# An encoder trunk of two layers on one core: the mLSTM gates as columns of the first value group, two norm rows through DRAM, and one PSUM tile per token half in the last block

## Chip, cores and metric

The kernel runs on one core of a Trainium2 chip. The metric is the device time of one execution in microseconds (us); lower is better.

## What is computed

The reference is a hybrid encoder of two layers over 256 tokens of width 2048, float32 in and out. Cut to what the change touches:

```python
for layer in range(2):
    h = rms_norm(x, norm_mix[layer])
    if layer % 2 == 0:   # pooling + grouped-query attention, one input and one output projection
        ...
    else:                # mLSTM, 8 heads of 256, forward and backward
        proj = h @ w_in_c                      # 2048 x (4 * 2048 + 32)
        q, k, v, o = four blocks of 2048 columns
        gates = proj[..., 4 * 2048:] + b_gate  # 32 columns: (i, f) x 2 directions x 8 heads
        # per head and direction: scores weighted with exp(cumulative gates), running maximum,
        # normalised, summed over both directions, RMSNorm per head, times sigmoid(o)
        mixed = y @ w_out_c
    x = x + mixed
    x = x + conv_ffn(rms_norm(x, norm_ffn[layer]), ...)   # 2048 -> 2 * 5632, conv of width 3, SiLU gate, 5632 -> 2048
```

## The kernel before

**Precision.** Every large product is done in float32r with split operands: a value is stored as a high part and a rest, and a product is high x high + high x rest + rest x high, accumulated in PSUM.

**Weights.** `Stream` (line 65) brings the weights in chunks of 128 x 1024 floats, in the order in which they are used: SP loads a chunk (line 78) up to five ahead into six buffers, ScalarE (ACT) writes its high part (line 87), VectorE (DVE) the rest (line 88), two chunks ahead into four buffers.

**Activations.** The residual `x` lies with tokens on partitions, in two halves t of 128 tokens. `Norm` (line 226) makes the transposed input `xx` of the next layer from it: after each 512 columns of the residual are final, `add` takes their squares on ACT and, some microseconds of PE work later, `block` transposes them on TensorE (PE, line 251) and writes high part and rest with the gain (lines 263, 266). The scale 1/rms is not multiplied into `xx` but into the products. `finish` (line 275) makes it in two shapes: `rcol`, one number per token with tokens on partitions (a power on GpSimd (POOL), line 207, and a few short steps on DVE), and `R`, the same numbers as a row on every partition: two diagonal matrices on DVE (`dg`, line 284), a product with ones on PE (`npr`, line 287) and a copy (line 289). There are four norms, numbered 0 to 3, two for each layer.

**Groups of products.** `stat_group` (line 292) keeps weights stationary and streams `xx`; per tile of 128 input rows k it issues two matmuls of 512 columns and two of 256. `mov_group` (line 331) keeps `xx` stationary and streams the weights, `width` columns at a time, six matmuls per k; it returns a PSUM tile from the pool `mm`, which has two. Small work of the heads (transposes, scores) uses the pool `ps` with four tiles.

**Order.** PE's instructions stand in program order, written by hand. `Weave` (line 109) puts the small steps between the matmuls of the groups: a step is a generator that says after how many microseconds of PE work it may go on, and every matmul group ticks that clock. Outside the first stage the order of ACT, DVE, POOL and SP is made by the framework's scheduler.

**mLSTM layer** (line 657). For each pair of heads hp: the values (`mv`, a moving group of 512 columns, line 841), scaled with `rcol` on ACT (line 844) and split; then for each of its heads q and k (`mq`, `mk`, stationary groups, scaled with `R` in `scaled`, line 735), and the output gates (`mo`). `gates` (line 686), added to the weave behind the first value group, has 32 matmuls of its own (`gps`): the 32 gate columns, spread to rows 0 to 103, stationary, in 16 tiles k with 512 and 256 streamed columns. Their weights are a load of their own, split on ACT and DVE into a tile cleared by POOL (lines 665 to 673). The gate rows [104, 256] get `R` and the bias, and then logarithms, running sums and maxima; the row for the heads goes to DRAM (`gd`, line 719) and each head fetches its part as a broadcast (`G`, line 757); two other rows are turned into columns on PE (`cols`, line 725). A head starts when `gate` is filled. In the attention layer `k_block` (line 548) runs `finish` of norm 0 as part of its steps; a power for the scales of k (`ry_qk`, line 207) stands between its two halves (line 436), and `R` is read by the pool groups (line 576).

**FFN layer** (line 870). `down` of the last chunk ends, for the last 512 columns, in `down_end` (line 903): one PSUM tile of both token halves; the last two k go half by half, the second half in two pieces of 256 columns, each added to the residual (line 925) and stored (line 926) as it is done.

Of the kernel before, what the change touches and what calls it, by code (L numbers as in the profile page):

```python
# [16 lines left out]
P = 128  # L17
# [47 lines left out]
class Stream:  # L65
# [8 lines left out]
    def load(self, pieces=1):  # L74
        i, n = self.n_load, CH * P // pieces
        w = self.wpool.tile([P, CH * P], F32, tag="w", name=f"w{i}")
        for c in range(0, CH * P, n):
            self.nc.sync.dma_start(w[:, c : c + n], self.srcs[i][:, c : c + n])
        self.w[i] = w, n
        self.n_load += 1  # L80

    def split(self, then=None):
        i = self.n_split
        w, n = self.w.pop(i)
        hl = self.spool.tile([P, 2, CH * P], F32R, tag="hl", name=f"hl{i}")
        for c in range(0, CH * P, n):
# [68 lines left out]
def trunk(ctx: ExitStack, tc: tile.TileContext, gx, xT, xn, call, catt, cml, wgate, weights, out):  # L155
# [12 lines left out]
    sm1 = pool("small1", 1)  # L168
    mmp = pool("mm", 2, space=PSUM)
# [56 lines left out]
    class Norm:  # L226


        def __init__(self, n):
# [3 lines left out]
            self.blocks, self.R = 0, None  # L233
# [41 lines left out]
        def finish(self):  # L275
# [5 lines left out]
            yield 2.5  # L281
            dg = sm1.tile([P, 2, P], F32, tag="dg", name=f"dg{n}")
# [48 lines left out]
    def mov_group(act, name, width=512, before=None, after=None):  # L331

        ps = mmp.tile([P, 2, width], F32, tag="mm", name=name)
        per = CH * P // width
        hl = None
        for k in range(KT):
# [9 lines left out]
            for t, i, j in terms:  # L346
                first, last = k == 0 and (width == 512 or t == 0), k == KT - 1 and (width == 512 or t == 1)
                mm(ps[:, t, :], src[:, i, t * P : t * P + P], hl[:, j, c : c + width],
                   first and i + j == 0, last and i == 1)
# [307 lines left out]
    def mlstm_layer(norm, nxt):  # L657
        with ExitStack() as es:
# [10 lines left out]
            g.memset(wgp.bitcast(F32), 0.0)  # L669
# [460 lines left out]
```

## Time and profile before

| | us |
|---|---|
| median of three runs | 2212.0 (2211.6 to 2212.02) |
| profiled execution | 2211.96 |
| its span, first to last instruction | 2209.7 |
| PE busy in the span | 2203.7 |
| DVE, ACT, POOL busy | 1527.5, 1169.1, 27.7 |

The granted clock of PE is 1.00 over the run. In the rows of the profile, L200 is the helper that issues matmuls, so groups are told apart by the tile that they write: `mv<-hl,xx` is the value group. A row of the timeline gives start, length, engine, line, operation, output and input, shapes, count, and in brackets the idle time before it with what ended it. PEld is the loading of the stationary operand, which overlaps PE. A matmul's length includes the drain that the next one overlaps, so lengths of single matmuls do not add up to time on PE.

### The profile page before, as it was taken

To read this page: it belongs to the slowest core of one execution; us is meant where nothing else is said; L and a number is where in the kernel's file an instruction comes from. 1 tells how busy PE (TensorE), PEld (TensorE's weight loads), DVE (VectorE), ACT (ScalarE), POOL (GpSimd) and SP (SyncE) were. 2 spreads that over 40 slices of the span, in tenths; PEclk is the share of its full clock that TensorE was granted. 3 is DMA by queue.
4 is the path that set the end of the run, shared out by engine and by line. 5 is a ranking of instruction groups with operands and counts; after the bars stand their busy time and mean duration, and the time that the engine had idled before them with its cause. 6 is when DMAs were issued, how large, how long until landed. Compare 5 with 4: busy or idle time off the path is not lost.

```text
span 2209.7 us, 30530 instructions
## 1 busy us (share of the span) xinstructions
PE 2203.7 (100%) x11656; PEld 1886.9 (85%) x11656; DVE 1527.5 (69%) x2180; ACT 1169.1 (53%) x1662; POOL 27.7 (1%) x36
## 2 busy tenths in 40 slices
PE   9999999999999999999999999999999999999999
PEld 7888888888888888888888889888888888888887
DVE  7686677776766767666777677667777677676764
ACT  7665555554554545455455554555555455454542
POOL 0020000000000000000000000000000000000000
PEclk9999999999999999999999999999999999999999
DMA  9455566656566566655565555655565656656564
GB/s 340 157 165 173 175 191 190 191 188 194 187 193 189 188 194 189 200 181 164 172 200 180 183 180 165 187 178 188 188 191 189 197 185 193 188 190 192 190 193 141
DMA packets 117876, 415.45 MB, mean 188 GB/s; under 512 B 12986, under 2 KB 15458, under 8 KB 117730
## 3 DMA queue, kind: packets, MB, share of 16 engines
q1 hardware_dynamic: 114512, 409.50, 58.1%
q10 hardware_dynamic: 3218, 4.01, 0.7%
q8 instruction: 91, 1.49, 0.3%
q14 instruction: 55, 0.45, 0.1%
HBM read 411.31 MB, written 2.14 MB: 187 GB/s over the span
## 4 chain that ended last, share of the span: by engine, by line
PE 99%; DMA 0%; DVE 0%; SPq 0%; ACT 0%; issue 0%
PE up L200 44%; PE dn L200 21%; PE op L200 8%; PE mk L200 4%; PE mq L200 4%; PE mo L200 4%; PE mv L200 4%; PE qproj L200 3%; PE pool L200 1%; PE vproj L200 1%; PE kproj L200 1%; PE end L200 1%; PE qk L200 1%; PE av L200 1%; PE xt L251 0%; PE ov L200 0%
## 5 line engine op out<-in xcount | busy, mean ns | idle before, releaser
L88 DVE TENSOR_TENSOR hl<-w,hl 128x1024 fp32r<-128x1024 f32 (+1 forms) x770 | 938.3, 1219 | 467.9 <-ACT hl L87 466.3
L87 ACT CAST hl<-w 128x1024 fp32r<-128x1024 f32 (+1 forms) x769 | 805.9, 1048 | 674.8 <-PE dn L200 240.9
L200 PE MATMUL up<-xx,hl 128*128 128x512 f32 (+1 forms) x5632 | 984.2, 337 | 0.0
L200 PEld LDWEIGHTS up<-xx,hl 128*128 128x128 f32 x5632 | 857.9, 188 | 125.9
L200 PE MATMUL dn<-hl,g 128*128 128x512 f32 x2064 | 471.3, 389 | 0.0
L200 PEld LDWEIGHTS dn<-hl,g 128*128 128x128 f32 x2064 | 386.2, 188 | 79.5
L356 ACT COPY tb_up<-up 128x512 f32<-128x512 f32 x88 | 51.7, 587 | 153.9 <-PE up L200 153.9
L357 DVE TENSOR_TENSOR tb_up<-up,tb_up 128x512 f32<-128x512 f32 x88 | 60.9, 691 | 97.0 <-ACT tb_up L356 97.0
L892 ACT ACTIVATE y<-tb_up,cst 128x256 f32<-128x256 f32 x176 | 96.4, 595 | 47.1 <-DVE tb_up L888 47.1
L200 PE MATMUL mk<-xx,hl 128*128 128x512 f32 (+1 forms) x512 | 92.4, 338 | 0.0
L200 PE MATMUL mq<-xx,hl 128*128 128x512 f32 (+1 forms) x512 | 92.0, 337 | 0.0
L200 PE MATMUL mo<-hl,xx 128*128 128x512 f32 (+1 forms) x480 | 91.6, 348 | 0.0
L200 PE MATMUL op<-hl,cat 128*128 128x512 f32 x384 | 91.6, 393 | 0.0
L200 PE MATMUL mv<-hl,xx 128*128 128x512 f32 x384 | 89.6, 391 | 0.0
L200 PE MATMUL op<-hl,mcat 128*128 128x512 f32 x384 | 89.5, 392 | 0.0
L200 PEld LDWEIGHTS mq<-xx,hl 128*128 128x128 f32 x512 | 79.3, 188 | 11.7
L200 PEld LDWEIGHTS mk<-xx,hl 128*128 128x128 f32 x512 | 79.1, 188 | 11.5
L200 PEld LDWEIGHTS mo<-hl,xx 128*128 128x128 f32 x480 | 76.5, 189 | 10.6
L200 PEld LDWEIGHTS mv<-hl,xx 128*128 128x128 f32 x384 | 71.7, 188 | 14.8
L200 PEld LDWEIGHTS op<-hl,mcat 128*128 128x128 f32 x384 | 71.4, 188 | 14.6
L200 PEld LDWEIGHTS op<-hl,cat 128*128 128x128 f32 x384 | 70.9, 188 | 14.1
L893 DVE SCALAR_TENSOR_TENSOR y<-tb_up,cst,y 128x255 f32<-128x255 f32 x176 | 76.7, 477 | 0.0
(211 smaller groups left out, 1285.1 us busy)
## 6 DMA issues: line engine op xcount, KB each, us to landing
w<-in_up SPq DMA_DIRECT2D x352, 512.0 KB, 4.0
w<-in_dn SPq DMA_DIRECT2D x176, 512.0 KB, 4.0
w<-in_m_in SPq DMA_DIRECT2D x128, 512.0 KB, 4.0
w<-in_a_in SPq DMA_DIRECT2D x46, 512.0 KB, 4.2
w<-in_a_out SPq DMA_DIRECT2D x32, 512.0 KB, 3.5
w<-in_m_out SPq DMA_DIRECT2D x32, 512.0 KB, 3.5
x<-in_xn SPq DMA_DIRECT2D x4, 512.0 KB, 9.3
G<-gd ACTq DMA_DIRECT2D x16, 128.0 KB, 4.9
```

The source lines that it names most:

```text
L87: (self.nc.vector.tensor_copy if i + c == 0 else self.nc.scalar.copy)(hl[:, 0, c : c + n], w[:, c : c + n])
L88: self.nc.vector.tensor_sub(hl[:, 1, c : c + n], w[:, c : c + n], hl[:, 0, c : c + n].bitcast(F32))
L200: pe.matmul(out_, lhsT, rhs, start=start, stop=stop, skip_group_check=True)
L356: a.copy(tb, ps[:, :, 1, :])
L357: v.tensor_add(tb, ps[:, :, 0, :], tb)
L892: a.activation(y[:, j, :], u[:, j, :], AF.Identity, scale=cw(tl, 1), bias=cw(tl, 3))
L893: v.scalar_tensor_tensor(y[:, j, 1:S], u[:, j, 0 : S - 1], cw(tl, 0), y[:, j, 1:S], ALU.mult, ALU.add)
```

## The change

- **Gates in the first value group.** The first value group (512 columns) becomes two moving groups: one of 288 columns, the first head's 256 value columns and the 32 gate columns, and one of 256, the second head's values. The tile of the first has 512 columns for each token half, of which 288 are used. Its weights come as chunks of 3 k x 288 = 864 columns (the last has one k, 288). `gates` then scales the gate columns with `rcol` on ACT into a cleared tile `gn`, turns them with two transposes on PE (`gtr`), and adds the bias; the rest of the chain is the same, and its wait before `cols` is 16 us of PE work instead of 13. The gates' own weights, their load, split, memset and 32 matmuls go. The clock steps of `finish` are 6 us instead of 8, and the weave is run until `rcol` exists before the evacuation.
- **Norm rows.** For norms 0 and 2, `R` is made by two DMAs on POOL's queue: `rcol` to a DRAM row, and the row back as a broadcast to 128 partitions. For norms 1 and 3 it stays as it was.
- **Last block.** `down_end` uses two PSUM tiles of the pool `ps`, one for each token half; the second half is done in one piece of 512 columns.

```diff
     def load(self, pieces=1):
-        i, n = self.n_load, CH * P // pieces
+        i = self.n_load
+        width = self.srcs[i].shape[-1]
+        n = width // pieces
...
             self.rcol = rsqrt(s2, 2, 1.0 / D, f"n{n}")
             yield 2.5
+            if n % 2 == 0:
+                rr = dram.tile([2, P], F32, tag="rr", name=f"rr{n}")
+                g.dma_start(rr.rearrange("t p -> p t"), self.rcol)
+                R = sm1.tile([P, S], F32, tag="R", name=f"R{n}")
+                g.dma_start(R.rearrange("p (t q) -> p t q", t=2), rr.unsqueeze(0).to_broadcast([P, 2, P]))
+                self.R = R
+                return
             dg = sm1.tile([P, 2, P], F32, tag="dg", name=f"dg{n}")
...
-            wgf = t1p.tile([P, KT, 4, MH], F32, tag="vf", name="wgf")
-            a.dma_start(wgf.rearrange("p k c h -> p k (c h)"), wgate)
-
-            wgp = actp.tile([P, KT, 2, P], F32R, tag="B0", name="wg")
-            g.memset(wgp.bitcast(F32), 0.0)
-            wg4 = wgp.rearrange("p k a (c h) -> p k a c h", c=4)[:, :, :, :, :MH]
-            a.copy(wg4[:, :, 0], wgf)
-            v.tensor_sub(wg4[:, :, 1], wgf, wg4[:, :, 0].bitcast(F32))
-            wg = wgp[:, :, :, :NGATE]
...
-            def gates():
-                ps = psp.tile([P, 2, S], F32, tag="ps", name="gps")[:NGATE]
-                for k in range(KT):
-                    src = norm.xx[:, k]
-                    mm(ps.rearrange("p a b -> p (a b)"), wg[:, k, 0, :], src.rearrange("p a b -> p (a b)"),
-                       k == 0, False)
-                    mm(ps[:, 1, :], wg[:, k, 1, :], src[:, 0, :], False, k == KT - 1)
+            def gates(ps):
+
+                gn = t1p.tile([P, 2, P], F32, tag="arg", name="gn")
+                g.memset(gn, 0.0)
+                for t in range(2):
+                    a.activation(gn[:, t].rearrange("p (c h) -> p c h", c=4)[:, :, :MH],
+                                 ps[:, t, MD : MD + 32].rearrange("p (c h) -> p c h", c=4),
+                                 AF.Copy, scale=norm.rcol[:, t : t + 1])
+                yield 3.0
+                tr = psp.tile([P, S], F32, tag="ps", name="gtr")[:NGATE]
+                for t in range(2):
+                    pe.transpose(tr[:, t * P : t * P + P], gn[:, t, :NGATE], ident)
                 pre = kp.tile([NGATE, S], F32, tag="pre", name="pre")
-                a.copy(pre, ps[:, 1, :])
-                v.tensor_add(pre, ps[:, 0, :], pre)
-                v.tensor_mul(pre, pre, norm.R[:NGATE])
-                v.tensor_scalar_add(pre, pre, kc[:NGATE, M_BG : M_BG + 1])
-                ra = t1p.tile([40, 4, S], F32, tag="vf", name="rows_a")
+                v.tensor_scalar_add(pre, tr, kc[:NGATE, M_BG : M_BG + 1])
+                ra = t1p.tile([40, 4, S], F32, tag="og", name="rows_a")
...
-                yield 13.0
+                yield 16.0
...
-            wv.add(norm.finish(), 8.0)
+            wv.add(norm.finish(), 6.0)
             for hp in range(MH // 2):
-                ps = mov_group(xx, f"mv{hp}")
                 vf = t1p.tile([P, 2, 512], F32, tag="vf", name=f"mvf{hp}")
-                for t in range(2):
-                    a.activation(vf[:, t, :], ps[:, t, :], AF.Copy, scale=norm.rcol[:, t : t + 1])
+                for c, n in ((0, MD + 32), (MD, MD)) if hp == 0 else ((0, 512),):
+                    ps = mov_group(xx, f"mv{hp}_{c}", n)
+                    if hp + c == 0:
+                        wv.until(lambda: norm.rcol is not None)
+                        wv.add(gates(ps))
+                    n = min(n, 512 if hp else MD)
+                    for t in range(2):
+                        a.activation(vf[:, t, c : c + n], ps[:, t, :n], AF.Copy, scale=norm.rcol[:, t : t + 1])
...
-                    wv.add(gates())
...
             def down_end(gt, b, kts):
 
-                ps = mmp.tile([P, 2, 512], F32, tag="mm", name="end")
+                parts = [(0, 0, 512), (1, 0, 512)]
+                pss = [psp.tile([P, 512], F32, tag="ps", name=f"end{i}") for i in range(2)]
...
-                for t, c0, c1 in ((0, 0, 512), (1, 0, 256), (1, 256, 512)):
+                for i, (t, c0, c1) in enumerate(parts):
                     for k in kts[-2:]:
-                        terms(t, k, hl, c0, c1)
+                        terms(i, k, hl)
                     xs = x[:, t, b * 512 + c0 : b * 512 + c1]
-                    v.tensor_add(xs, xs, ps[:, t, c0:c1])
+                    v.tensor_add(xs, xs, pss[i][:, : c1 - c0])
                     nc.sync.dma_start(out[:, t, b * 512 + c0 : b * 512 + c1], xs)
```

More of the change, by code (lines that the diff above doesn't have):

```diff
@@ L83, in split @@
         i = self.n_split
-        w, n = self.w.pop(i)
+        w, n, width = self.w.pop(i)
         hl = self.spool.tile([P, 2, CH * P], F32R, tag="hl", name=f"hl{i}")
-        for c in range(0, CH * P, n):
+        for c in range(0, width, n):
             (self.nc.vector.tensor_copy if i + c == 0 else self.nc.scalar.copy)(hl[:, 0, c : c + n], w[:, c : c + n])
@@ L154, in trunk @@
 @with_exitstack
-def trunk(ctx: ExitStack, tc: tile.TileContext, gx, xT, xn, call, catt, cml, wgate, weights, out):
+def trunk(ctx: ExitStack, tc: tile.TileContext, gx, xT, xn, call, catt, cml, weights, out):
     nc = tc.nc
@@ L168, in trunk @@
     sm1 = pool("small1", 1)
+    dram = pool("nd", 2, space=bass.MemoryType.DRAM)
     mmp = pool("mm", 2, space=PSUM)
@@ L232, in __init__ @@
             self.ss = smp.tile([P, 2, NB], F32, tag="nss", name=f"nss{n}")
-            self.blocks, self.R = 0, None
+            self.blocks, self.R, self.rcol = 0, None, None
         def at(self, k):
@@ L331, in mov_group @@
     def mov_group(act, name, width=512, before=None, after=None):
-        ps = mmp.tile([P, 2, width], F32, tag="mm", name=name)
+        ps = mmp.tile([P, 2, 512 if width > 256 else width], F32, tag="mm", name=name)
         per = CH * P // width
@@ L346, in mov_group @@
             for t, i, j in terms:
-                first, last = k == 0 and (width == 512 or t == 0), k == KT - 1 and (width == 512 or t == 1)
-                mm(ps[:, t, :], src[:, i, t * P : t * P + P], hl[:, j, c : c + width],
+                first, last = k == 0 and (width > 256 or t == 0), k == KT - 1 and (width > 256 or t == 1)
+                mm(ps[:, t, :width], src[:, i, t * P : t * P + P], hl[:, j, c : c + width],
                    first and i + j == 0, last and i == 1)
```

31 lines of the change are left out of this document (19 added, 12 removed).

## The prediction

> **What bounds the kernel now.** I read the page first: its part on busy time, then the chain of work that ended last.
>
> ```profile
> span 2209.7 us, 30530 instructions
> PE 2203.7 (100%) x11656; PEld 1886.9 (85%) x11656; DVE 1527.5 (69%) x2180; ACT 1169.1 (53%) x1662; POOL 27.7 (1%) x36
> PE 99%; DMA 0%; DVE 0%; SPq 0%; ACT 0%; issue 0%
> ```
>
> TensorE (PE) is busy from end to end and the chain is PE in 99%. The other engines have a third or more of the span free. So a microsecond of matmul removed is a microsecond gained, and one added is lost, as long as no operand comes late. Next the view of waits, for PE alone (engine, line, what it waited for: total, times, longest):
>
> ```profile
> PE end L200 <- DVE x L925: 1.3, 2, 0.8
> PE wps L224 <- DVE pad L585: 1.2, 1, 1.2
> ```
>
> PE waits in two places only: at the very start, and twice in the last block, which the change touches. Everything else in this prediction is a count of PE time, plus the question whether a new operand arrives after PE wants it. For the count I need the pace of back-to-back matmuls, start to start. A row's own mean time (some 390 ns for 512 columns) contains the drain that the next matmul covers, so I divide the distance between neighbouring rows by their counts; from the chain in order of time and from the timeline of PE:
>
> ```profile
> 391.89 21.77 PE dn L200 x96
> 413.67 89.16 PE up L200 x512
> ...
> 1355.88 7.35 PE L200 MATMUL mo<-hl,xx 128*128 128x256 f32 x60
> 1363.07 1.12 PE L200 MATMUL qk<-hl_k,hl_q 128*128 128x256 f32 x8
> ```
>
> 512 columns: (413.67 - 391.89)/96 = 226.9 ns. 256 columns: (1363.07 - 1355.88)/60 = 119.8 ns. Half the columns cost 53%, so there are some 13 ns per matmul beside the columns.
>
> **The change, part by part.** First the gates and the first value group, in the timeline around 1000 us (start, length, engine, line, operation, count):
>
> ```profile
> 990.67 4.25 PE L200 MATMUL mv<-hl,xx 128*128 128x512 f32 x18
> ...
> 994.76 0.60 PE L251 MATMUL xt<-cst,x 128*128 128x128 f32 x4
> ...
> 995.11 1.64 PE L200 MATMUL mv<-hl,xx 128*128 128x512 f32 x6
> ...
> 996.94 8.44 PE L200 MATMUL mv<-hl,xx 128*128 128x512 f32 x36
> ...
> 1000.04 0.48 DVE L266 SCALAR_TENSOR_TENSOR xx<-xt,gcol,xx 128x256 fp32r<-128x256 f32 x1 [0.54 <-ACT xx L263]
> ...
> 1005.22 0.60 PE L200 MATMUL npr<-dg,cst 128*128 128x256 f32 x2
> ...
> 1013.86 0.85 PE L200 MATMUL mq<-xx,hl 128*128 128x512 f32 x4
> ...
> 1014.55 5.71 PE L200 MATMUL gps<-xx,wg 128*104 128x512 f32 x32
> 1020.10 10.62 PE L200 MATMUL mq<-xx,hl 128*128 128x512 f32 x60
> ```
>
> Gate matmuls (gps): 32 go. mq resumes at 1020.10, so they hold PE for 1020.10 - 1014.55 = 5.55 us. **-5.55.** (16 pairs of 512 and 256 columns at the paces above would be 5.55 too: loading 104 columns of weights instead of 128 changes nothing, so at these widths the columns streamed set the pace and not the weight load.)
>
> First value group (mv0): 96 matmuls of 512 columns become 96 of 288 and 96 of 256. No row has 288 columns. Its pace lies between the rows of 256 and 512, 119.8 and 226.9; I take the straight line, 119.8 + 32/256 x 107.1 = 133.2 ns, because the cost beside the columns was the same in both. Added: 96 x (133.2 + 119.8 - 226.9) = **+2.5 us**; with the ends for 288, +1.2 and +11.5. [...]
>
> Two transposes of the gate columns (gtr) are new. Four transposes (xt) move the next matmul by 995.11 - 994.76 = 0.35, so two cost 0.18; the six matmuls behind a group of xt take 0.1 more than their pace, which I add: **+0.27**.
>
> Norm rows: the product npr goes for the norms of the attention and the mLSTM. From 996.94 to 1013.86 are 16.92 us for 72 mv matmuls (72 x 0.2269 = 16.34), the 0.1 behind the transposes, and npr: 0.48. Two of them: **-0.95**.
>
> The gate columns of the heads (cols):
>
> ```profile
> 1034.32 0.42 ACT L716 ACTIVATE rows_b<-rows_b 40x256 f32<-40x256 f32 x1
> ...
> 1034.83 0.96 PEld L200 LDWEIGHTS cols<-cst,rows_b 40*128 40x128 f32 x8
> ```
>
> Now the exponent is done at 1034.74 and PE starts on it at once; I read 0.1 us of hidden wait. Afterwards the gate rows start some 10 us earlier: **-0.1**.
>
> The end:
>
> ```profile
> 2193.42 9.68 PE L200 MATMUL end<-hl,g 128*128 128x512 f32 x42
> ...
> 2203.14 0.69 DVE L925 TENSOR_TENSOR x<-x,end 128x512 f32<-128x512 f32 x1 [7.10 <-PE end L200]
> ...
> 2203.88 0.98 PE L200 MATMUL end<-hl,g 128*128 128x256 f32 x6 [0.78 <-DVE x L925]
> ...
> 2205.37 0.97 PE L200 MATMUL end<-hl,g 128*128 128x256 f32 x6 [0.51 <-DVE x L925]
> 2206.38 0.42 DVE L925 TENSOR_TENSOR x<-x,end 128x256 f32<-128x256 f32 x1 [1.06 <-PE end L200]
> ```
>
> PE waits for an addition that reads the other half of the same PSUM tile: its last matmul ends at 2206.34 and the last addition at 2206.80. With a tile per half the remaining 6 matmuls of 512 follow on: 2193.42 + 47 x 0.2269 + 0.39 = 2204.47. The addition is then 128x512, 0.69 us by the row of the first half, and ends at 2205.20, 1.6 us earlier. The last store doubles to 256 KB. From the rows of the stores (KB each, us to landing):
>
> ```profile
> out<-x SPq DMA_DIRECT2D x1, 512.0 KB, 3.0
> out<-x SPq DMA_DIRECT2D x2, 128.0 KB, 1.7
> ```
>
> a third of the 1.3 us between them is 0.4. The end gives 1.6 - 0.4 = **-1.2**.
>
> Costed at nothing, from the groups of the split weights between 990 and 1014 us, the gates' timeline, the group of the output-gate activations, and the timeline again:
>
> ```profile
> 996.50 0.16 DVE L212 TENSOR_TENSOR re_n<-re_n,ry_n 128x2 f32<-128x2 f32 x1
> ...
> L88 DVE TENSOR_TENSOR hl<-w,hl x9: 1217/1224/1226, 989.2 to 1012.4; 128x1024 fp32r<-128x1024 f32 x9
> L87 ACT CAST hl<-w x8: 1043/1055/1056, 990.9 to 1011.3; 128x1024 fp32r<-128x1024 f32 x8
> ...
> L814 ACT ACTIVATE og<-mo,nrcol x10: 464/687/697, 1094.4 to 1383.8; 128x512 f32<-128x512 f32 x6, 128x256 f32<-128x256 f32 x4
> ...
> 1002.70 1.05 ACT L87 CAST hl<-w 128x1024 fp32r<-128x1024 f32 x1 [1.67 <-PE mv L200]
> ```
>
> The gate weights' own load, split and memset go (ACT, DVE and POOL, none of them late). The first six weight chunks are 864 or 288 columns wide instead of 1024; PE stays on 18 matmuls of 133 ns for 2.4 us where it stayed 2.7 on a chunk, and the splits (1.22 us of DVE, 1.05 of ACT for 1024 columns) shrink with them. SP issues two more loads. The transposed input is needed sooner: tile k=12 at 990.67 + 72 x 0.1332 + 0.9 = 1001.2, and the last of the four is ready at 1000.52 (row L266 above), so 0.6 us are left in the worst case; beyond it PE would wait one for one. The first part ends at 1004.4; ACT then scales two value halves of 256 columns (0.46 each) and two short gate pieces, some 1.5 us, and gtr is wanted 36 matmuls later, at 1008.7: 2.5 us of cover. The scale itself is ready at 996.7. The R row through DRAM is first read when mq has ended, near 1028, and in the attention by the pool groups, behind three more projections. A 512 KB store lands after 3.0 us by the row above, so two small trips of 5 us each would still leave 20.
>
> Sum: -5.55 + 2.5 + 0.27 - 0.95 - 0.1 - 1.2 = **-5.0 us**. The profiled execution took 2211.96 (span 2209.7 and 2.3 around it), the median of the runs is 2212.0, so the forecast is 2207.0.
>
> **The rivals.** *POOL's queue* (still faster, but by less). POOL issues no DMA in this profile. In the attention the store of the norm goes ahead of ry_qk, for which DVE waits already:
>
> ```profile
> 44.59 0.15 DVE L212 TENSOR_TENSOR re_n<-re_n,ry_n 128x2 f32<-128x2 f32 x1
> ...
> 45.70 1.64 POOL L207 TENSOR_TENSOR ry_qk<-rv_qk,mhalf 128x8 f32<-128x8 f32 x1 [3.78 <-DVE rv_qk L205]
> ...
> 47.38 0.17 DVE L209 TENSOR_TENSOR re_qk<-ry_qk 128x8 f32<-128x8 f32 x1 [0.40 <-POOL ry_qk L207]
> ...
> 48.44 1.23 DVE L88 TENSOR_TENSOR hl<-w,hl 128x1024 fp32r<-128x1024 f32 x1 [0.48 <-ACT hl L87]
> ...
> 49.97 1.29 DVE L440 TENSOR_TENSOR rot_k<-rot_k,re_qk 128x512 f32<-128x512 f32 x2
> ...
> 52.60 0.60 PE L449 MATMUL tr_k<-cst,rot_k 128*128 128x128 f32 x4
> ```
>
> Behind ry_qk stand the k scales, rot_k and the weight splits on DVE, then tr_k on PE. rot_k ends 1.34 us before tr_k, and DVE idles 0.48 on the way, so ry_qk may end at 49.16 instead of 47.34 before PE notices: the store, starting at 44.8, may hold POOL for 49.16 - 1.64 - 44.8 = 2.7 us. Nearest rows:
>
> ```profile
> 1032.45 0.54 ACTq L719 DMA_DIRECT2D gd<-gr  x1
> ...
> L669 POOL MEMSET wg<- x1: 3532/3532/3532, 944.5 to 944.5; 128x4096 f32 x1
> ```
>
> An issue on ACT's queue takes 0.54, the longest POOL operation 3.5. I take under 2.7, a small transfer being nearer to the former; with 3.5 PE waits 0.8 (2207.8), and with twice that 4.3 (2211.3). [...]
>
> *288 columns cost like 512* (slower than before). Place: the 96 matmuls of the first value part. Price: 96 x (226.9 - 133.2) = 9.0 us, so 2216.0. It decides from a pace of 133.2 + 5000/96 = 185 ns. For it: no row has a width between. Against: gps and mo show 256 columns at just over half.
>
> *Late operands in the first value group*: the faster consumption (2.4 us a chunk, one chunk of a single k) or gtr uncovers ACT or the transposes, with cover of 0.6 and 2.5 us. A miss of one ACT copy and one DVE split is 2.3 us: 2209.3. For it: every chunk's copy starts when PE frees a buffer (1002.70 above), so PE's pace is handed on without a reserve. Against: that copy had sat idle 1.67 us before it, and the chunks shrink with the pace.
>
> *The end does not change*: if PE still waited for DVE in the last block, 1.2 us stay: 2208.2. For it: the waits in that list are put down to the addition, not to the tile. Against: the 128x256 pieces read disjoint columns, so only the shared tile is left to tie them.
>
> **How the numbers follow.** Forecast 0.66 (2205.8 to 2208.0), POOL's queue 0.11 (2207.8 to 2211.3), late operands 0.10 (2208.5 to 2211), end unchanged 0.07 (2208.2), slow 288 columns 0.06 (2212 to 2216; the upper half of the bound for 288). The range 2205.6 to 2210.8 leaves out the slow columns, the tails of the stalls and of the forecast, some 0.13 in all. 0.2% is 4.4 us, about what a measurement of this kernel can tell from no change; 2207.6 is its edge and the forecast is 0.6 inside. Faster by more: nine tenths of the forecast, 0.59; within: the rest of it and the three middle cases, 0.34; slower by more, about 0.07, from slow columns and the worst of the stalls.
>
> **What would show it.** Rows of mv with 128x288 at 133 ns start to start, gps and two npr gone, the mq group starting near 1016; no PE wait for DVE in the last block, the last addition 128x512 ending near 4.5 us before the span's end minus what the larger store takes; PE's list of waits with the start alone in it. Wrong would be: PE waiting for ACT or DVE between 990 and 1030 us or at tr_k, a store on POOL over 2.7 us, a pace of 288 columns well off the line, or a store of 256 KB that takes over 1 us more than one of 128 KB.

## The result, and the profile after

| | before | after |
|---|---|---|
| median, us (lowest to highest, runs) | 2212.09 (2211.6 to 2212.61, 10) | 2206.64 (2206.46 to 2206.75, 10) |
| profiled execution | 2211.96 | 2206.69 |
| its span | 2209.7 | 2204.4 |

The ratio is 0.9975, 95% interval 0.9965 to 0.9985. The forecast was 2207.0. The page of the changed kernel, its busy time and its chain:

```profile
span 2204.4 us, 30654 instructions
...
PE 2199.3 (100%) x11712; PEld 1888.3 (86%) x11712; DVE 1525.3 (69%) x2172; ACT 1168.8 (53%) x1666; POOL 28.1 (1%) x40
...
PE 100%; DVE 0%; issue 0%
```

PE has 56 matmuls more and 4.4 us less of busy time. Its list of waits now has the start alone:

```profile
PE wps L227 <- DVE pad L595: 1.2, 1, 1.2
```

The timeline around the gates (lines of the code have moved by some ten; L203 is the helper for matmuls now):

```profile
990.15 4.12 PE L203 MATMUL mv<-hl,xx 128*128 128x288 f32 x30
...
994.11 0.60 PE L254 MATMUL xt<-cst,x 128*128 128x128 f32 x4
...
995.70 12.49 PE L203 MATMUL mv<-hl,xx 128*128 128x288 f32 x96
...
996.10 0.80 POOL L287 DMA_DIRECT2D rr<-re_n  x1 [2.28 <-DVE nrcol L858]
...
997.80 0.48 DVE L269 SCALAR_TENSOR_TENSOR xx<-xt,gcol,xx 128x256 fp32r<-128x256 f32 x1 [0.54 <-ACT xx L266]
...
1004.84 0.47 ACT L692 ACTIVATE gn<-mv,re_n 128x32 f32<-128x32 f32 x2
...
1006.12 0.57 POOL L289 DMA_DIRECT2D R<-rr  x1 [9.23 <-DMA rr<-re_n]
...
1008.02 0.38 PE L698 MATMUL gtr<-cst,gn 128*104 128x128 f32 x2
...
1008.16 7.43 PE L203 MATMUL mv<-hl,xx 128*128 128x256 f32 x60
...
1015.43 10.61 PE L203 MATMUL mq<-xx,hl 128*128 128x512 f32 x60
...
1030.73 0.68 DVE L740 SCALAR_TENSOR_TENSOR tb_q<-tb_q,R 128x512 f32<-128x512 f32 x1
```

Read the paces off the distances: 288 columns (994.11 - 990.15)/30 = 132 ns, 256 columns (1015.43 - 1008.16)/60 = 121 ns. The row of 96 mixes 60 of the one and 36 of the other. The value group with its two groups of transposes took 1013.86 - 990.67 = 23.19 us before and takes 1015.43 - 990.15 = 25.28 now; the 5.55 us of gps behind it are gone.

The end, in the timeline:

```profile
2189.45 11.04 PE L203 MATMUL end<-hl,g 128*128 128x512 f32 x48
...
2199.16 0.69 DVE L935 TENSOR_TENSOR x<-x,end 128x512 f32<-128x512 f32 x1 [7.10 <-PE end L203]
...
2200.53 0.69 DVE L935 TENSOR_TENSOR x<-x,end 128x512 f32<-128x512 f32 x1 [0.67 <-PE end L203]
```

PE issues its 48 matmuls without a gap. By the unrounded trace (span 2204.41 us, before 2209.66) the last addition ends at 2201.21, 3.20 us ahead of the span's end; before, it ended at 2206.80, 2.85 ahead.

By stages, from the start of the first matmul of each in the two traces: start -0.15 us, attention layer -0.38, first FFN 0.00, mLSTM layer -3.45, second FFN 0.00, last block -1.27; together the 5.25 us between the spans.

### The profile page after: what moved, and what is told of

Its sections match the earlier page's. It is cut to its first block, busy times and chain, and to the rows that moved or that the text cites. A ratio compares the mean times of both kernels' runs of the same rounds, so it can differ in the third digit from the quotient of the medians.

```text
span 2204.4 us, 30654 instructions
## 1 busy us (share of the span) xinstructions
PE 2199.3 (100%) x11712; PEld 1888.3 (86%) x11712; DVE 1525.3 (69%) x2172; ACT 1168.8 (53%) x1666; POOL 28.1 (1%) x40
## 4 chain that ended last, share of the span: by engine, by line
PE 100%; DVE 0%; issue 0%
PE up L203 44%; PE dn L203 21%; PE op L203 8%; PE mv L203 4%; PE mq L203 4%; PE mk L203 4%; PE mo L203 4%; PE qproj L203 3%; PE kproj L203 1%; PE pool L203 1%; PE vproj L203 1%; PE qk L203 1%; PE av L203 1%; PE end L203 0%; PE xt L254 0%; PE sc L203 0%
## 5 line engine op out<-in xcount | busy, mean ns | idle before, releaser
L90 DVE TENSOR_TENSOR hl<-w,hl 128x1024 fp32r<-128x1024 f32 (+2 forms) x772 | 939.0, 1217 | 467.9 <-ACT hl L89 466.2
L203 PE MATMUL up<-xx,hl 128*128 128x512 f32 (+1 forms) x5632 | 984.2, 337 | 0.0
L203 PEld LDWEIGHTS up<-xx,hl 128*128 128x128 f32 x5632 | 857.9, 188 | 125.8
L203 PE MATMUL dn<-hl,g 128*128 128x512 f32 x2064 | 471.3, 389 | 0.0
L203 PEld LDWEIGHTS dn<-hl,g 128*128 128x128 f32 x2064 | 386.3, 188 | 79.4
L203 PE MATMUL mk<-xx,hl 128*128 128x512 f32 (+1 forms) x512 | 92.2, 337 | 0.0
L203 PE MATMUL mq<-xx,hl 128*128 128x512 f32 (+1 forms) x512 | 92.1, 337 | 0.0
L203 PE MATMUL mv<-hl,xx 128*128 128x512 f32 (+2 forms) x480 | 91.7, 350 | 0.0
L203 PE MATMUL mo<-hl,xx 128*128 128x512 f32 (+1 forms) x480 | 91.6, 348 | 0.0
L203 PE MATMUL op<-hl,cat 128*128 128x512 f32 x384 | 91.6, 393 | 0.0
L203 PE MATMUL op<-hl,mcat 128*128 128x512 f32 x384 | 89.5, 392 | 0.0
L203 PEld LDWEIGHTS mq<-xx,hl 128*128 128x128 f32 x512 | 79.2, 188 | 11.6
L203 PEld LDWEIGHTS mk<-xx,hl 128*128 128x128 f32 x512 | 79.0, 188 | 11.4
L203 PEld LDWEIGHTS mv<-hl,xx 128*128 128x128 f32 x480 | 78.3, 189 | 11.2
L203 PEld LDWEIGHTS mo<-hl,xx 128*128 128x128 f32 x480 | 76.5, 190 | 10.6
L203 PEld LDWEIGHTS op<-hl,mcat 128*128 128x128 f32 x384 | 71.4, 188 | 14.6
L203 PEld LDWEIGHTS op<-hl,cat 128*128 128x128 f32 x384 | 70.9, 188 | 14.1
```

The source lines that it names most:

```text
L90: self.nc.vector.tensor_sub(hl[:, 1, c : c + n], w[:, c : c + n], hl[:, 0, c : c + n].bitcast(F32))
L203: pe.matmul(out_, lhsT, rhs, start=start, stop=stop, skip_group_check=True)
```

## The experiments

The theory is that of the prediction: PE's path is a count of matmuls at paces set by their columns, each part of the change gives its own term whether it stands alone or not, and the DMAs on POOL's queue hide. The rivals: gains that overlap or appear elsewhere, a queue that is only just covered, and another rule for the price of a matmul.

### The parts alone

**Only the last block.** The edit to the kernel before:

```diff
-                ps = mmp.tile([P, 2, 512], F32, tag="mm", name="end")
+                parts = [(0, 0, 512), (1, 0, 512)]
+                pss = [psp.tile([P, 512], F32, tag="ps", name=f"end{i}") for i in range(2)]
```

> The kernel before with only the last block changed (two PSUM tiles, second half in one piece). Theory A (the gain is a sum of PE time, each part worth its own count, and the end is worth the two waits for the addition): the last matmul ends 1.9 us earlier, the last addition 1.6 us earlier, the last store costs 0.3 more (2.90 us from the last addition's end to the span's end before, 3.18 in the changed kernel), so 1.3 us less than before. Rival B (the waits were put down to the wrong thing; only the shapes count): 6 wide matmuls for 12 narrow ones save 0.1, the larger addition and store cost 0.6, so 0.5 us more than before.

Measured: 2210.78 (2210.22 to 2210.95, 11 runs), 1.31 less than before; ratio 0.9994 (0.9985 to 1.0003). Alone a part is too small for the interval, but the trace is plain: PE's two waits of 1.3 us in the last block are gone, and the block is 1.38 us shorter. This run changed both the tiles and the width of the last piece; further down, pieces of 256 columns come back in tiles of their own and bring no wait, so it was the shared PSUM tile that tied PE to the addition.

**Only the norm rows.** To the kernel before:

```diff
+            if n % 2 == 0:
+                rr = dram.tile([2, P], F32, tag="rr", name=f"rr{n}")
+                g.dma_start(rr.rearrange("t p -> p t"), self.rcol)
...
+                return
```

> The kernel before with only the norm rows 0 and 2 through DRAM on POOL's queue. Theory A (a product with ones costs PE its own 0.25 us and 0.2 more on the matmul behind it, and nothing waits for the row): 0.9 us less than before. Rival B (only its own 0.25 us counts): 0.5 less. Rival C (the store on POOL's queue ahead of the power for k, or the late row, holds PE): no gain or a loss, with a PE wait near 50 or 1030 us.

Measured: 2211.13 (2210.99 to 2211.26), -0.96; ratio 0.9996 (0.9987 to 1.0005). The attention layer is 0.49 shorter, the mLSTM layer 0.49. That is the 0.48 that the prediction read for one npr, twice. PE has one new wait, 0.15 us at 12 us, in the first stage, which this edit does not touch; near 50 and 1030 us, where rival C looked, there is none.

**Only the gates.** The changed kernel, with the norm rows and the last block as before:

```diff
-            if n % 2 == 0:
-                rr = dram.tile([2, P], F32, tag="rr", name=f"rr{n}")
...
-                return
...
-                pss = [psp.tile([P, 512], F32, tag="ps", name=f"end{i}") for i in range(2)]
+                ps = mmp.tile([P, 2, 512], F32, tag="mm", name="end")
```

> The changed kernel with the old norm rows and the old last block: the gates as columns of the first value group alone. Theory A (PE time: 5.55 us of gate matmuls go, 96 x (133.9 + 120.7 - 227.1) = 2.6 come, transposes 0.27 come, 0.1 at cols goes): 2.8 us less than before. Rival B (part of the gain comes from the gate chain being early, or from the other parts together with this one, so that parts do not add): clearly off 2.8, by over 0.5 either way.

Measured: 2208.32 (2208.21 to 2208.51), -3.77; ratio 0.9983 (0.9974 to 0.9992). The gain is larger than the 2.8 expected, by enough to meet rival B's sign, but not in the place of the change: the mLSTM layer is 3.01 shorter. The rest lies outside it: 0.17 at the start, 0.12 in the last block, 0.29 around the span (2.01 us here, 2.30 in the kernel before, unrounded), and the medians stand 0.17 further apart than the profiled executions. So the three medians (-1.31, -0.96, -3.77) sum to 6.04 where the whole change gave 5.45, while the mLSTM layer adds up: -3.01 - 0.49 = -3.50 against -3.45.

**Only the narrower group.** The kernel before, with its first value group as two of 256 columns and the gates left as they were:

```diff
-                ps = mov_group(xx, f"mv{hp}")
+                for c, n in ((0, MD), (MD, MD)) if hp == 0 else ((0, 512),):
+                    ps = mov_group(xx, f"mv{hp}_{c}", n)
```

> The kernel before with the first value group as two moving groups of 256 columns and the gates left as they were: the price of the split alone. Theory A (some 13 ns per matmul beside the columns, 96 matmuls more): 96 x (2 x 119.8 - 226.9) = 1.2 us more than before. Rival B (weights of the narrow groups come late, or evacuation delays the next group): over 2 us more, with PE waits between 990 and 1030 us. Rival C (the weave moves steps so that something else gains): no more than before.

Measured: 2212.83 (2212.62 to 2213.3), +0.74; ratio 1.0004 (0.9995 to 1.0013). The group, in the timeline:

```profile
990.74 3.75 PE L200 MATMUL mv<-hl,xx 128*128 128x256 f32 x30
994.34 0.60 PE L251 MATMUL xt<-cst,x 128*128 128x128 f32 x4
...
1015.06 0.86 PE L200 MATMUL mq<-xx,hl 128*128 128x512 f32 x4
```

The pace is (994.34 - 990.74)/30 = 120 ns and the group takes 24.32 us, 1.13 more; the whole layer is 1.17 longer, against 1.2 expected. The time shows less because only 1.9 us lie around the span in 8 of the 11 executions here.

### POOL's queue

In the attention layer of the changed kernel:

```profile
44.91 0.88 POOL L287 DMA_DIRECT2D rr<-re_n  x1 [3.13 <-DVE qss_k L435]
...
45.57 1.23 DVE L90 TENSOR_TENSOR hl<-w,hl 128x1024 fp32r<-128x1024 f32 x1 [0.36 <-ACT hl L89]
...
45.81 2.51 POOL L210 TENSOR_TENSOR ry_qk<-rv_qk,mhalf 128x8 f32<-128x8 f32 x1
...
48.35 0.17 DVE L212 TENSOR_TENSOR re_qk<-ry_qk 128x8 f32<-128x8 f32 x1 [1.56 <-POOL ry_qk L210]
...
50.38 1.29 DVE L450 TENSOR_TENSOR rot_k<-rot_k,re_qk 128x512 f32<-128x512 f32 x2
...
52.45 0.60 PE L459 MATMUL tr_k<-cst,rot_k 128*128 128x128 f32 x4
```

The store holds POOL 0.88 us, ry_qk behind it takes 2.51 instead of 1.64 and ends at 48.32, 0.98 later. DVE's idle time takes half of that up (rot_k 0.41 later), and rot_k still ends 0.8 before tr_k.

ry_qk starts only 0.11 later, at 45.81 instead of 45.70; the other 0.87 is its length, and that goes with a weight split on DVE. Here ry_qk starts 0.25 us into the split of 45.57 and ends 1.53 after that split's end; in the kernel before, it started 0.01 ahead of its split and took 1.64. What the store does is to hold POOL past 45.57, since ry_qk's operand is ready at 45.20. In all nine kernels with the store on POOL's queue, ry_qk starts inside a split and ends 1.53 to 1.54 us behind it. Two powers without any DMA on POOL do the same: `ry_qk` of the run with the last block alone takes 2.73 us beside a split that starts 3 ns after it, and `ry_qq` of the run on ACT's queue (below) takes 2.54:

```profile
64.32 1.22 DVE L90 TENSOR_TENSOR hl<-w,hl 128x1024 fp32r<-128x1024 f32 x1
...
64.49 2.54 POOL L210 TENSOR_TENSOR ry_qq<-rv_qq,mhalf 128x8 f32<-128x8 f32 x1 [17.66 <-DVE rv_qq L208]
```

What was not expected either stands in the DMA list (KB each, us to landing):

```profile
R<-rr POOLq DMA_DIRECT2D x2, 128.0 KB, 6.5
...
rr<-re_n POOLq DMA_DIRECT2D x2, 1.0 KB, 9.6
```

A store of 1 KB lands after 9.6 us, three times as late as one of 512 KB on SP's queue (3.0 in the prediction). To see whether its late row costs anything, and whether the queue makes it late, all four norms got it:

```diff
-            if n % 2 == 0:
+            if True:
```

> The changed kernel with all four norm rows through DRAM on POOL's queue, not two. In the changed kernel a store of a norm row landed 9.2 to 9.6 us after its issue and the fetch 6.5 after its own, so a row is there some 16 us after the scale. In front of the FFN the scale is ready near 262.4 and VectorE wants the row at 270.1. Theory A (rows cost nothing only where the cover is longer than these 16 us; here VectorE stands for some 8 us, the weight splits behind it stop, and PE runs dry after two chunks of 2.8 us): two products less save 0.9, two stalls of 3 to 5 us are paid, 2212 to 2216, with PE waits for the split weights near 275 and 1490 us. Rival B (the row is never on the path): 2205.7.

Measured: 2209.88 (2208.08 to 2215.82, 11 runs), ratio 0.9992 (0.9983 to 1.0001). PE's waits and the timeline of the second FFN:

```profile
PE up L203 <- DVE hl L90: 2.9, 2, 2.1
```

```profile
1486.26 0.57 POOL L289 DMA_DIRECT2D R<-rr  x1 [7.96 <-DMA rr<-re_n]
...
1490.83 0.69 DVE L895 TENSOR_TENSOR tb_up<-tb_up,R 128x512 f32<-128x512 f32 x1 [6.33 <-DMA R<-rr]
```

There `R` is read by the first tile of the FFN. DVE stands 6.33 us for it with the weight splits queued behind (7.7 in the first FFN), and PE waits 2.9 us for splits in the two FFNs, 2.1 of them in the first. Two npr are saved (-0.96) and the time is 3.2 up, with a spread of 7.7 us where the changed kernel has 0.3; the four longest of the 11 executions, 2210.46 and more, are those with a mean granted clock under 1.00 (0.998 or 0.999). The mechanism is the expected one, its price lower. The row through DRAM pays in the two norms with a long way to the first reader, and not in the other two: in the mLSTM layer of the changed kernel the read lands 5.9 us after its issue, at 1012.0, and its reader starts 1030.73 - 1012.0 = 18.7 us later.

The same with all four on ACT's queue:

```diff
-                g.dma_start(rr.rearrange("t p -> p t"), self.rcol)
+                a.dma_start(rr.rearrange("t p -> p t"), self.rcol)
```

(and the read likewise).

> The changed kernel with all four norm rows through DRAM, issued on ACT's queue instead of POOL's. The gate rows go the same way on that queue: their fetch is issued 1.6 us after the store and lands after 5.4. Theory A (on this queue the row is there some 7 us after the scale, in time for VectorE in front of the FFN, and ACT's wait for the store, about 1.6 us, fits in its idle time): 0.9 us less than the changed kernel, 2205.7. Rival B (ACT's wait or a late row in front of the FFN uncovers PE): over 2206.6, with PE waits near 270 and 1490 us. Rival C (the slow store is due to its many 4-byte pieces and not to the queue, so it takes 9 us here too and ACT stands as long): 2 to 8 us more than the changed kernel.

Measured: 2214.56 (2211.78 to 2219.65, 11 runs), ratio 1.0013 (1.0004 to 1.0021). The DMA list, the waits, PE's timeline and the engines by windows (after the stretch and its length: PE, PEld, DVE, ACT and POOL busy, granted clock, DMA share, GB/s):

```profile
R<-rr ACTq DMA_DIRECT2D x4, 128.0 KB, 5.2
...
rr<-re_n ACTq DMA_DIRECT2D x4, 1.0 KB, 9.0
```

```profile
ACT hl L89 <- DMA rr<-re_n: 10.2, 1, 10.2
...
1009.88 0.58 PE L203 MATMUL mv<-hl,xx 128*128 128x256 f32 x1 [5.15 <-ACT hl L89]
...
1008.30:1015.00 6.70, 4.44 (x19) 4.15 (x20) 4.72 (x4) 4.96 (x8) 0.00 (x0) 0.50 0.69 125
```

Theory A falls, and rival C holds in its price. The store is as late on this queue, 9.0 us, so it is not POOL's queue that makes it late (what fewer pieces do, the next run shows); and the read, which waits for the store, stands in ACT's queue ahead of the weight splits. ACT stood still 10.2 us and PE 5.1, both in the first value group, not in front of the FFN. On POOL that wait has nothing behind it: in the changed kernel POOL stands 6.58 and 9.23 us for the two stores, and its next row after each read waits another 7.37 and 52.98 us for its own operand.

This wait of PE cost more than its length. Near its end the granted clock falls to 0.50, and it stays there from 1008.2 to 1015.0 us, where matmuls of 256 columns start 213 ns apart: the 36 from 1009.88 to 1017.12 take 7.24 us instead of 36 x 0.1207 = 4.35, and only 0.68 of that is a second wait. The half clock adds an estimated 2.2 us to the 5.1 (7.24 - 4.35 - 0.68). All 11 executions have a mean clock of 0.997 to 0.999.

Two more small stores and their reads, which nothing uses, in the norms that keep the product: 128 pieces of 8 bytes (`pr`) and 128 of 4 bytes (`ph`).

```diff
+            if n == 1:
+                g.dma_start(pr, self.rcol)
+                g.dma_start(pb, pr)
+            else:
+                g.dma_start(ph.rearrange("t p -> p t"), self.rcol[:, 0:1])
+                g.dma_start(pb[0:1, 0:2], ph[:, 0:2])
```

> The changed kernel with two more small stores and reads on POOL's queue that nothing uses, in the two norms that keep the product: 128 pieces of 8 bytes (both token halves of one partition side by side) in one, 128 pieces of 4 bytes (one token half) in the other, beside the 256 pieces of 4 bytes of the norm rows that land after 9 to 10 us. Theory A (cost per piece, on top of the 2 us of a plain store): 2 + 128 x 7/256 = 5.5 us for both. Rival B (a fixed price of a tiny store on this queue): 9 us for both. Rival C (cost per element of 4 bytes): 9 for the pieces of 8 bytes, 5.5 for the other.

```profile
rr<-re_n POOLq DMA_DIRECT2D x2, 1.0 KB, 9.1
pr<-re_n POOLq DMA_DIRECT2D x1, 1.0 KB, 6.0
ph<-re_n POOLq DMA_DIRECT2D x1, 0.5 KB, 7.4
pb<-ph POOLq DMA_DIRECT2D x1, 0.0 KB, 4.3
```

128 pieces land after 6.0 and 7.4 us, one transfer each, 256 after 9.1: fewer pieces are sooner, as A has it, and neither B nor C fits. But 8 bytes read back take 4.3 us. If a store has the same fixed part, it is some 4 us and not 2, and a piece is an estimated (9.1 - 4.3)/256 = 19 ns, which gives 6.7 us for 128 pieces; these few transfers do not settle it. The time, 2206.45 in one run, is that of the changed kernel.

### The last block in finer pieces

```diff
-                parts = [(0, 0, 512), (1, 0, 512)]
+                parts = [(0, 0, 512), (1, 0, 256), (1, 256, 512)]
```

> The changed kernel with three PSUM tiles in the last block, the second half as two pieces of 256 columns in tiles of their own. Theory A (what is left at the end is PE time plus the last addition and store): 24 matmuls of 512 become 48 of 256, 24 x (2 x 119.8 - 226.9) = 0.3 more; the last addition is 0.27 shorter and the last store 0.3: 0.2 to 0.3 less than the changed kernel, 2206.4, and no PE wait in the last block. Rival B (pieces of 256 bring the waits back whatever the tile): 1 us more than the changed kernel.

Measured: 2206.23 (2206.08 to 2206.38, 8 runs), ratio 0.9974 (0.9963 to 0.9984). No wait of PE comes back. From the first to the last matmul of the block it is 11.13 us instead of 10.65, from there to the span's end 3.54 instead of 4.31: 0.30 less together, the upper end of what theory A expects. Next, only the last two k of the second half are split, and the rest of it is added early:

```diff
+                parts = [(0, 0, 512), (1, 0, 512), (1, 0, 256), (1, 256, 512)]
...
+                add(1)
+                for i in (0, 2, 3):
```

> The changed kernel, with four PSUM tiles in the last block: the first token half whole, the first six k of the second half in one 512-column tile that is added to the residual early, and only its last two k in two tiles of 256 columns, each added and stored as it is done. Theory A (PE waits only for an addition that reads the tile it writes; half the columns cost 53%): against three tiles (2206.23), where all 24 matmuls of the second half were split, only the last 6 are: 6 x (2 x 0.1207 - 0.2271) = 0.09 us of PE instead of 24 x 0.0143 = 0.34, so 0.25 us less, 2206.0, and no wait of PE in the last block. Rival B (the early addition of the second half, 0.69 us on DVE, delays the others or makes PE wait): the last additions come late and the time is 2206.3 to 2206.9.

```profile
2189.47 11.11 PE L203 MATMUL end<-hl,g 128*128 128x512 f32 x54
...
2199.19 1.13 DVE L928 TENSOR_TENSOR x<-x,end 128x512 f32<-128x512 f32 x2 [0.67 <-PE end L203]
...
2200.61 0.42 DVE L928 TENSOR_TENSOR x<-x,end 128x256 f32<-128x256 f32 x1 [0.30 <-PE end L203]
```

Measured: 2205.90 (2205.57 to 2206.47, 8 runs), ratio 0.9972 (0.9962 to 0.9983); theory A's 2206.0. The matmuls take 10.83 us and the tail 3.53. This is the best version found; it beats the kernel before, and stands 0.74 us below the changed one, with 0.60 of it in the rows of the last block. The intervals of the ratios overlap, so against the changed kernel the rows carry this, not the times.

### What a narrow matmul costs

The prediction priced a matmul by its columns and 13 ns. That makes 27 ns for 32 columns, and gates as a group of their own would cost the same 2.6 us as 288 columns in the value group:

```diff
-                for c, n in ((0, MD + 32), (MD, MD)) if hp == 0 else ((0, 512),):
-                    ps = mov_group(xx, f"mv{hp}_{c}", n)
+                ps = mov_group(xx, f"mv{hp}")
...
+                if hp == 0:
+                    wv.add(gates(mov_group(xx, "mg", 32)))
```

> The changed kernel, but the first value group stays 512 columns wide and the 32 gate columns are a moving group of their own behind it, 96 matmuls of 32 columns. Theory A (a matmul costs its columns plus 13 ns; the load of the stationary operand stays hidden at any width): 96 x 27 ns = 2.6 us, the same as the 96 x (133.9 + 120.7 - 227.1) = 2.6 us that the gates cost in the changed kernel, so 2206.6. Rival B (below some width the load of the stationary operand sets the pace; the shortest pace in the rows is that of the transposes with 128 columns, 0.35 / 4 = 88 ns): 96 x 88 ns = 8.4 us, 5.8 more, 2212.4; at the mean length of a load, 188 ns, it would be 18 us and 2222.

Measured: 2223.1 (2221.78 to 2223.46, 4 runs), ratio 1.0049 (1.0035 to 1.0062); 16.5 us over the changed kernel. The timeline of PE, and the engines by windows (after the span: PE, PEld, DVE, ACT and POOL busy, granted clock, DMA share, GB/s):

```profile
1013.09 15.57 PE L203 MATMUL mg<-hl,xx 128*128 128x32 f32 x96
1028.51 6.09 PE L203 MATMUL mq<-xx,hl 128*128 128x512 f32 x24
```

```profile
1013.00:1018.00 5.00, 5.00 (x47) 4.96 (x45) 2.36 (x2) 3.15 (x4) 0.00 (x0) 1.00 0.42 129
1018.00:1023.00 5.00, 5.00 (x28) 5.00 (x27) 0.00 (x0) 0.00 (x0) 0.00 (x0) 0.55 0.29 96
1023.00:1028.40 5.40, 5.40 (x27) 5.40 (x27) 0.00 (x0) 0.00 (x0) 0.00 (x0) 0.50 0.00 0
1028.50:1032.00 3.50, 3.50 (x11) 2.98 (x12) 1.23 (x1) 1.40 (x3) 0.00 (x0) 0.50 0.00 0
1032.00:1036.00 4.00, 4.00 (x25) 3.49 (x24) 1.62 (x2) 1.08 (x2) 0.00 (x0) 0.98 0.39 131
```

Theory A falls twice. In the first window the clock is full and the weight loads fill the time (PEld 4.96 of 5.00): the first 49 matmuls start 112 ns apart by the trace, not 27 (which the very first pair shows). Then the clock drops to 0.50, though PE counts as busy throughout, and the other 46 start 213 ns apart; it is back only 3.5 us into the next group. In sum, 96 x (112 - 27) = 8.2 us for the loads, 15.42 - 96 x 0.112 = 4.7 for the clock in the group, and 1.7 behind it, where ten matmuls of mq take 3.56 us instead of 6 x 0.233 + 4 x 0.115: 14.6 of the 15.1 by which the span grew. (The profiled execution is the shortest of the four.)

That rival B's second price, 2222, lies near the time is luck: it has every load at 188 ns and a full clock. The same spacing stands in the trace of the kernel before, where the eight matmuls of `cols` with 40 columns start 111 to 112 ns apart and the transposes xt with 128 columns 108; the 88 ns of the expectation divide by four a stretch whose last step is 27 ns, to a matmul that pays for its load in a row 0.09 us longer.

A load's own row is no measure of that spacing: it lasts 187 to 192 ns (mg of the next kernel) and 138 to 144 (xt of the kernel before), where the matmuls start 112 and 108 ns apart. In the run on ACT's queue the half clock came with a wait of PE of 5.15 us; here no row of PE is idle, and PE only streams 32 columns in a time in which, by the paces of 256 and 512 columns, an estimated 240 would have fitted ((112 - 13)/0.418 ns).

To part load and clock, each narrow matmul was put behind a wide one with the same stationary operand:

```diff
+                if extra is not None:
+                    mm(extra[:, t, :], src[:, i, t * P : t * P + P], hl[:, j, width : width + 32],
+                       k == 0 and t == 0 and i + j == 0, k == KT - 1 and t == 1 and i == 1)
```

> The changed kernel with the first value group 512 columns wide and, behind each of its 96 matmuls, one of the 32 gate columns with the same stationary operand, into a PSUM tile of its own; a chunk of the stream is one k of 544 columns. In the kernel with the 96 narrow matmuls in a row they started 112 ns apart at a granted clock of 1.00 and, after 5.3 us, 213 ns apart at 0.50. Theory A (each stationary load needs some 112 ns of its own after the matmul before it has started, and the clock fell because TensorE streamed too little): a pair takes 227 + 112 ns, so the gates cost 96 x 112 = 10.8 us where the changed kernel pays 2.6; the clock stays at 1.00; 2206.6 + 8.1 = 2214.8. Rival B (a load is hidden behind a wide matmul further ahead, so only the average counts): a pair takes 227 + 27, the time is 2206.6. Rival C (narrow matmuls as such bring the clock down): 0.50 in part of the group, 2220 and more.

```profile
1001.15 0.18 PE L203 MATMUL mg<-hl,xx 128*128 128x32 f32 x1
1001.18 0.48 PE L203 MATMUL mv<-hl,xx 128*128 128x512 f32 x1
1001.50 0.18 PE L203 MATMUL mg<-hl,xx 128*128 128x32 f32 x1
```

Measured: 2215.35 (2215.12 to 2215.55, 10 runs), ratio 1.0015 (1.0006 to 1.0025); theory A's 2214.8. A pair takes 344 ns by the trace, 117 more than the wide one alone, and the granted clock is 1.00 in all of the stretch from 990.2 to 1024.0, so neither rival B nor C fits: it is not narrow matmuls as such that bring the clock down. That too little streaming did it, as theory A has it, is not shown: no run varies its share in steps.

The rows show where the time goes. The load for a wide matmul starts only when the narrow one ahead of it has started (3 ns later by the trace) and takes its 188 ns; the wide row starts 27 ns behind the narrow one, but it is 0.48 us long where others of 512 columns are 0.39, and the next narrow one starts 317 ns behind it, not 227. In these rows a load hides behind the one matmul ahead of it, and where that has 32 columns, the next narrow one starts 90 ns later.

### The cover of the transposes

```diff
-                yield 3.0
+                yield 0.0
```

> The changed kernel with the two transposes of the gate columns placed 24 matmuls of 256 columns (2.9 us) earlier. Theory A (the scaled gate columns are done at 1005.3 us and the transposes start at 1008.0, a cover of 2.5 to 2.7 us): PE waits once, 0.2 to 0.5 us, for ACT's gn, and the time is 2206.9. Rival B (the semaphore or the evacuation takes longer than the row shows, the cover is smaller than it looks): a wait of 1 us or more. Rival C (the weave's tick already holds the transposes back to another place): no wait and no change.

```profile
1004.62 0.47 ACT L692 ACTIVATE gn<-mv,re_n 128x32 f32<-128x32 f32 x2
...
1004.96 0.50 PE L698 MATMUL gtr<-cst,gn 128*104 128x128 f32 x2
1005.21 10.31 PE L203 MATMUL mv<-hl,xx 128*128 128x256 f32 x84
```

The matmuls behind gtr start 0.25 us after it, where it is 0.14 in the changed kernel: a wait of 0.1 us, a little under theory A's 0.2 to 0.5. The cover of the changed kernel is thus some 2.8 us. The time was 2206.55 in one run.

## Why the prediction held, step by step

- **What bounds it.** PE alone, before and after. No wait came in place of the ones that went.
- **Gates and first value group.** -5.55 for gps is exact, since the whole group went. The straight line between 256 and 512 columns held: 133 ns for 288 and 120 for 256 between most starts. The group is 2.09 us longer with one npr (0.48) gone, so the added columns and gtr cost 2.57, for 2.5 + 0.27. The mLSTM layer came out at -3.45, where the terms, gtr, one npr and cols included, make -3.36.
- **The gate columns of the heads.** The -0.1 is not there: the eight matmuls of cols hold PE for 1035.84 - 1034.83 = 1.01 us before and 1026.98 - 1025.97 = 1.01 now. There was no hidden wait; the matmuls of 40 columns, each with a load of its own, start 111 to 112 ns apart (the first two 133) in both traces. The layer's sum came out near because the group was 0.2 us cheaper than its terms; that the two errors offset each other is luck.
- **The rival of 288 columns at the price of 512** was far off: 132 ns against the 185 from which it decides. A price that the columns do not set does show, on the other side of the rows: the 112 ns between matmuls of 32 and of 40 columns. The step "at these widths the columns streamed set the pace and not the weight load" is right for its widths, 256 and 512; 256 columns, at 120 ns, are only 8 ns above the 112, which the prediction did not see, though xt (108 ns) and cols (112) show it in the trace of before.
- **Norm rows.** -0.96 alone, for -0.95; in the whole change the attention layer gave 0.38 of its 0.48. The other 0.1 belongs to this one execution: the same layer took 227.89 to 228.15 us in the nine profiled kernels with the row on POOL's queue, with 228.15 in the changed kernel, and 228.53 before.
- **POOL's queue.** Held: the store has POOL for 0.88 us, of the 2.7 allowed, and ry_qk ends 0.98 late, of 49.16 - 47.34 = 1.82. But 0.87 of the 0.98 comes from starting inside a weight split, a cost that the prediction did not count. The step that failed without harm is "two small trips of 5 us each would still leave 20": the trips took 10.0 (996.10 to the read's issue at 1006.12) and 5.9, and left 18.7.
- **Late operands.** Held. The cover for `xx` was given as 0.6 us, from the time of the kernel before for the last tile, 1000.52; it is ready at 998.28 now and is wanted at 1000.4 (990.15 + 72 x 0.133 + 0.7 for two groups of transposes), so 2.1 us are left. The transposes come 1.25 us sooner with the faster matmuls (995.34, before 996.59); the rest of the 2.2 us is gained behind them, on ACT and DVE. For gtr the prediction's own figures leave 1008.7 - 1004.4 - 1.5 = 2.8 us of cover, not the 2.5 that it gives, and 2.8 is what the run with the earlier transposes showed.
- **The end.** -1.27 for -1.2. The larger store costs 3.20 - 2.85 = 0.35 us, for 0.4. The sign "near 4.5 us before the span's end" counts from the old end (2209.7 - 2205.2); in the new span it is the 3.20.
- **The sum.** -5.25 in the spans, for -5.0: 0.15 at the start, 0.07 in the last block, 0.09 in the mLSTM layer, less the 0.1 of the attention layer. The start differs by up to 0.5 us among all these kernels, whose first stage is the same, so the 0.15 is luck.
- **The chances.** "Slower by more" was fed from the slow 288 columns, but their own price ends at 2216.0, inside the edge of 2212.0 + 4.4 = 2216.4.

## What to carry to other kernels

Where one engine fills the span, count its instructions by the start-to-start distance of the same shape, and put the doubt into operands that come late. In these runs 32 columns more in a matmul of 256 that was there anyway cost 12 ns (132 against 120); as 96 matmuls of their own they started 112 ns apart at the full clock and 213 at a granted clock of 0.50, and the run was 16.5 us longer. A wait of PE of 5.15 us came with a clock of 0.50 too, and cost an estimated 2.2 us beyond its length. A wait for a DMA cost what was queued behind it on its engine (10.2 us of ACT with the weight splits behind it held PE for 5.1; 9.23 us of POOL cost PE none): give it to the engine with nothing behind, and only where the reader is further off than the two trips (10.0 and 5.9 us in the mLSTM layer).

## What the runs showed of the hardware that was not expected

- A 1 KB store of 256 pieces of 4 bytes lands after 8.2 to 9.9 us on POOL's queue and 8.4 to 11.5 on ACT's, one of 512 KB in long rows after 3.0 on SP's.
- With a load of the stationary operand each, matmuls in a row start 111 to 112 ns apart at full clock with 32 and 40 columns; a row of those with 32 brought the granted clock from 1.00 to 0.50 within 5.5 us, and it came back 3.5 us into the wide ones behind. A wait of PE of 5.15 us came with 0.50 as well, from 1008.2 to 1015.0 us.
- A power of 128x8 on POOL that starts inside a weight split on DVE ends some 1.5 us behind that split, and so takes 2.43 to 2.54 us instead of 1.64, with a DMA on POOL's queue or without.
- The two kernels with all four rows through DRAM, on POOL's queue and on ACT's, scatter by 7.7 and 7.9 us, and their longer executions show a lower mean clock (0.997 to 0.999); the others scatter by 0.3 to 1.7.
- The time around the span is 2.2 to 2.5 us in some executions and 1.8 to 2.1 in others, also of one kernel (1.92 to 2.50 with the last block alone). Nothing here tells why, and it is half a microsecond that no term of a sum explains.
